# A decoder layer on eight cores: from tile-by-tile through all stages to three passes over the sequence

## The chip, the cores and the metric

The kernel runs on all 8 cores of one Trainium2 chip, two dies of four cores (0 to 3 and 4 to 7). Each core works on half a sequence: 32 blocks of 128 tokens, and one block before them (the halo) that the attention and the pooling look back on. The metric is the device time in microseconds of the slowest core.

The runs also show a slower state: the granted TensorE clock is lower, mostly on one die, and the run is longer (in one run after 2931 us against 2684, with one die at a clock of 0.828 to 0.856 and the other at 0.935 to 0.961). Runs are therefore marked fast or slow.

## The reference, cut to what matters

```python
D_MODEL, BATCH, SEQ, D_FF = 1024, 4, 8192, 2816      # WINDOW = BLOCK = 128

mod = (silu(c) @ w_ada + b_ada).reshape(b, 9, 1024)  # shift, scale, gate of 3 sub-layers
# FFN, half step
h = modulate(x, sh1, sc1)                            # LayerNorm * (1 + scale) + shift
y = (silu(h @ w_gate) * (h @ w_up)) @ w_down
x = layer_norm(ALPHA * x + 0.5 * g1 * y, ln1_g, ln1_b)
# mixer: sliding-window attention with sinks, beside causal pooling over 2, 4, 8, 16 tokens
h = modulate(x, sh2, sc2)
x = layer_norm(ALPHA * x + g2 * token_mix(h), ln2_g, ln2_b)
# FFN, half step, with its own weights
h = modulate(x, sh3, sc3)
x = layer_norm(ALPHA * x + 0.5 * g3 * swiglu(h), ln3_g, ln3_b)
```

Inputs and weights are float32. In both kernels all large multiplications are in bfloat16.

## The kernel before

A helper records each operation with the buffers that it reads and writes, and turns that into semaphore waits. Each engine carries out its own operations in the recorded order (in e1 below VectorE stood 52.3 us behind one load). Below, PE stands for TensorE (matmuls; PEld are its weight loads), DVE for VectorE, ACT for ScalarE, POOL for GpSimd and SP for SyncE, which here only issues transfers. HBM is the memory that the inputs and the `scr_` copies lie in (492 MB were read from it). PSUM is the memory that the matmuls write to (the tiles `ps`, `tp` and `modps` of the profile); an operation of another engine that reads a result out of it is called an evacuation.

The kernel takes a tile of four blocks (512 tokens) through all three sub-layers before the next tile. Stage A is the first FFN (of the next tile), L the mixer, C the second FFN.

```python
order = [("A", 0)]
for t in range(NT):                      # NT = 9: the halo block, then 8 tiles
    if t + 1 < NT:
        order.append(("A", t + 1))
    order.append(("L", t))
    if t > 0:
        order.append(("C", t))
```

The kernel does not keep the weights of the three stages on chip together: every stage loads its own. At the start they are cast to bfloat16 copies in HBM. From there the gate/up weights go through a ring of two buffers. The down weights and the mixer weights take turns in one region.

```python
def issue_gu(upto):                      # gate/up: 1 MB per group, 11 groups per stage
    ...
    P.op("sp", lambda e, ...: e.dma_start(out=wgu[s][:], in_=scr_gu[f][j]), ...)
def load_wd_slot(f, j): ...              # down: 0.5 MB, 11 per stage
def load_mixer_w(): ...                  # 4.5 MB per tile
...
def cast_dma(dst, src, sem, bufs):       # f32 in HBM -> bf16 in HBM
    P.op("pool", lambda e, ...: e.dma_start(out=dst, in_=src), writes=bufs, dma=sem)
```

The attention mask is added before exp by a second matmul into the same PSUM buffer:

```python
e.matmul(ps[pb]..., lhsT=kT[...], rhs=qT_v[...], start=True, stop=False)
return e.matmul(ps[pb]..., lhsT=ident_bf[:], rhs=masks[:, mi, :]..., start=False, stop=True)
...
P.op("act", lambda e, ...: e.activation(out=E_v[iE][:, kv, jj, :], in_=ps[pb][:], func=AF.Exp, scale=0.125), ...)
```

The softmax here doesn't subtract the row's maximum and nothing guards it: scores larger than these inputs give would overflow.

Of the kernel before, what the change touches and what calls it, by code (L numbers as in the profile page):

```python
# [12 lines left out]
D = 1024  # L13
FF = 2816
NFC = 22
NGRP = 11
SEQ = 8192
NB_OWN = 32
TOK_OWN = 4096
TOK_IN = TOK_OWN + 128  # L20
# [3 lines left out]
NEG = -30000.0  # L24
POOL_WINDOWS = (2, 4, 8, 16)
ENG = ("pe", "act", "dve", "pool", "sp")

class Buf:
    def __init__(self, name, overlaps=()):
        self.name = name  # L30
        self.last_w = None
        self.readers = {}
        self.overlaps = list(overlaps)

class Prog:
    def __init__(self, nc, es):
        self.nc = nc
        self.es = es
        self.sems = {}
        for e in ENG:  # L40
            self.sems[e] = es.enter_context(nc.semaphore("s_" + e))
        self.cnt = {e: 0 for e in ENG}
        self.dcnt = {}
        self.q = {e: [] for e in ENG}
        self.waited = {e: {} for e in ENG}

    def new_sem(self, name):
        self.sems[name] = self.es.enter_context(self.nc.semaphore(name))
        self.dcnt[name] = 0
        return name  # L50

    def op(self, eng, fn, reads=(), writes=(), dma=None, waits=()):
        need = {}

        def add(ev):
            if ev is None:
                return
            k, v = ev
            if need.get(k, 0) < v:
                need[k] = v  # L60
# [3 lines left out]
        for b in writes:  # L64
            add(b.last_w)
            for k, v in b.readers.items():
                add((k, v))
            for o in b.overlaps:
                add(o.last_w)
                for k, v in o.readers.items():  # L70
                    add((k, v))
# [3 lines left out]
        for k, v in need.items():  # L75
            if k == eng and eng == "pe":
                continue
            if self.waited[eng].get(k, 0) >= v:
                continue
            self.waited[eng][k] = v  # L80
            wl.append((k, v))
# [15 lines left out]
    def flush(self, block):  # L97
        qs = self.q
        self.q = {e: [] for e in ENG}
        sems = self.sems  # L100

        def mk(eng):
            def body(e):
                for wl, fn, ev in qs[eng]:
                    for k, v in wl:
                        e.wait_ge(sems[k], v)
                    ins = fn(e)
                    ins.then_inc(sems[ev[0]], 1 if ev[0] in ENG else 16)
# [7 lines left out]

def build_program():
# [4 lines left out]

    x_c = din("x_c", [TOK_IN, D])
    c_c = din("c_c", [128, 8])
    w_ada = din("w_ada", [D, 9 * D])
    b_ada = din("b_ada", [1, 9 * D])
    wg = [din("ffn1_w_gate", [D, FF]), din("ffn2_w_gate", [D, FF])]
    wu = [din("ffn1_w_up", [D, FF]), din("ffn2_w_up", [D, FF])]
    wdn = [din("ffn1_w_down", [FF, D]), din("ffn2_w_down", [FF, D])]
    lng_d = [din("ln1_g", [1, D]), din("ln2_g", [1, D]), din("ln3_g", [1, D])]  # L130
    lnb_d = [din("ln1_b", [1, D]), din("ln2_b", [1, D]), din("ln3_b", [1, D])]
    w_in = din("w_in", [D, 1280])
    sinks_d = din("sinks_b", [128, 8])
    wmix_d = din("pool_w_mix", [4, 128, 128])
    pscale_d = din("pool_scale_p", [128, 4])
    w_out = din("w_out", [D, D])
    ident_bf_d = din("ident_bf", [128, 128], BF16)
    ident_f_d = din("ident_f", [128, 128])
    masks_d = din("masks", [128, 3, 128], BF16)
    amat_d = din("amat", [128, 16, 128], BF16)  # L140
    out_c = nc.dram_tensor("out_c", [TOK_OWN, D], F32, kind="ExternalOutput").ap()

    scr_gu = [nc.dram_tensor(f"scr_gu{f}", [NGRP, 128, 8, 2, 256], BF16).ap() for f in range(2)]
    scr_d = [nc.dram_tensor(f"scr_d{f}", [128, NFC, D], BF16).ap() for f in range(2)]
    scr_win = nc.dram_tensor("scr_win", [128, 8, 1280], BF16).ap()
    scr_woa = nc.dram_tensor("scr_woa", [128, 4, D], BF16).ap()
    scr_wop = nc.dram_tensor("scr_wop", [128, 4, D], BF16).ap()

    with ExitStack() as es:
        P = Prog(nc, es)  # L150

        def sb(name, shape, dt=F32, stack=es):
            return stack.enter_context(nc.sbuf_tensor("t_" + name, list(shape), dt))

        ident_bf = sb("ident_bf", [128, 128], BF16)
        ones_bf = sb("ones_bf", [128, 64], BF16)
        masks = sb("masks", [128, 3, 128], BF16)
        amat = sb("amat", [128, 16, 128], BF16)
        wmix = sb("wmix", [128, 4, 128], BF16)
        pscale = sb("pscale", [128, 4])  # L160
        sinkexp = sb("sinkexp", [128, 8])
        sinkb = sb("sinkb", [128, 4, 128])
        lng = [sb(f"lng{i}", [128, D]) for i in range(3)]
        lnb = [sb(f"lnb{i}", [128, D]) for i in range(3)]
        gate3 = sb("gate3", [128, D])
        msc = sb("msc", [128, 6, 8])

        B_const = Buf("const")
        B_gates = Buf("gates")
        B_msc = Buf("msc")  # L170
        B_sink = Buf("sink")

        s_const = P.new_sem("d_const")

        with ExitStack() as pes:
            ct = sb("ct", [128, 8], F32, pes)
            ident_f = sb("ident_f", [128, 128], F32, pes)
            cs = sb("cs", [128, 8], F32, pes)
            crep = sb("crep", [128, 8, 128], BF16, pes)
            ones_f = sb("ones_f", [1, 128], F32, pes)  # L180
            bada = sb("bada", [1, 9 * D], F32, pes)
            modb = sb("modb", [128, 9 * D], F32, pes)
            wada_t = [sb(f"wada{i}", [128, 8, 256], BF16, pes) for i in range(4)]
            dtmp = sb("dtmp", [128, 8, 128], F32, pes)
            gates = [sb(f"gate{i}", [128, D], F32, pes) for i in range(3)]
            stg_in = [sb(f"stg_in{i}", [128, 2, D], F32, pes) for i in range(3)]
            stg_out = [sb(f"stg_out{i}", [128, 2, D], BF16, pes) for i in range(3)]
            B_si = [Buf(f"si{i}") for i in range(3)]
            B_so = [Buf(f"so{i}") for i in range(3)]
            s_si = [P.new_sem(f"d_si{i}") for i in range(3)]  # L190
            s_so = [P.new_sem(f"d_so{i}") for i in range(3)]
            modps = [pes.enter_context(nc.psum_tensor(f"modps{i}", [128, 512], F32)) for i in range(2)]
            B_modps = [Buf(f"modps{i}") for i in range(2)]
            B_wada = [Buf(f"wada{i}") for i in range(4)]
            s_wada = [P.new_sem(f"d_wada{i}") for i in range(4)]
            B_modb = Buf("modb")
            B_misc = Buf("misc")
            B_dtmp = Buf("dtmp")

            cast_fam = {"gu0": [], "gu1": [], "win": []}  # L200
            for f in range(2):
                cast_ops = cast_fam[f"gu{f}"]
                for j in range(NGRP):
                    for gu, wsrc in enumerate((wg[f], wu[f])):
                        src = wsrc.rearrange("(kc p) (j n) -> j p kc n", p=128, n=256)[j]
                        dst = scr_gu[f][j][:, :, gu, :]
                        cast_ops.append((dst, src))
            cast_fam["wd2"] = []
            for j in range(NGRP):
                cast_fam["wd2"].append((scr_d[1][:, 2 * j:2 * j + 2, :],  # L210
                                        wdn[1].rearrange("(fc p) d -> p fc d", p=128)[:, 2 * j:2 * j + 2, :]))
            w_in_v = w_in.rearrange("(kc p) n -> p kc n", p=128)
            cast_ops = cast_fam["win"]
            cast_ops.append((scr_win[:, :, 512:1280], w_in_v[:, :, 512:1280]))
            for kc in range(8):
                for half in range(2):
                    src = w_in[kc * 128:(kc + 1) * 128, half * 256:(half + 1) * 256].rearrange("p (c d) -> p c d", d=64)
                    dst = scr_win[:, kc, 0:512].rearrange("p (c h d) -> p c h d", h=2, d=64)[:, :, half, :]
                    cast_ops.append((dst, src))
            cast_ops.append((wmix[:], wmix_d.rearrange("g c d -> c g d")))  # L220
            const_loads = [
                (ident_bf[:], ident_bf_d), (ident_f[:], ident_f_d), (masks[:], masks_d), (amat[:], amat_d),
                (pscale[:], pscale_d), (sinkexp[:], sinks_d), (ct[:], c_c), (bada[:], b_ada),
            ]
            for i in range(3):
                const_loads.append((lng[i][:], lng_d[i].partition_broadcast(128)))
                const_loads.append((lnb[i][:], lnb_d[i].partition_broadcast(128)))
# [302 lines left out]
        def drain():  # L530
            while live:
                tick()
# [375 lines left out]
```

## Time and profile before

| | before |
|---|---|
| time, median of 3 runs | 3764.38 us (3759.59 to 3768.85) |
| granted clock, median of each die | 0.861, 0.863 |
| PE busy | 70% of the span |

The page of the profiled execution: first the PE's busy time with its share and number of instructions, then rows of 40 equal slices of the span. Each digit is a share in tenths (9 is 90% or more); PEclk is the granted TensorE clock.

```profile
PE 2633.0 (70%) x12252; PEld 1204.5 (32%) x12252; DVE 1025.5 (27%) x1807; ACT 939.4 (25%) x1560; POOL 360.0 (10%) x284
...
PE   5601247478489858986799669966997699759567
...
PEclk9997568789699978997899879987998799879778
DMA  9869999942044304430443134313341235113122
```

The first eight slices, 750 us, have full DMA rows and gaps in PE. After them PE and its clock rise and fall with every tile.

The busy table by stage of the same core. The columns are the stretch in us, its length, busy us and instruction count of PE, PEld, DVE, ACT, POOL, then the granted clock, the share of the DMA engines and GB/s. The first five rows are one steady tile (A: gate/up, down; L; C: gate/up, down); the last two are the start.

```profile
core 3: us, PE busy (x) PEld busy (x) DVE busy (x) ACT busy (x) POOL busy (x), PEclk, DMA share, GB/s
1174.00:1252.00 78.00, 71.15 (x320) 31.47 (x320) 15.71 (x23) 13.67 (x22) 4.55 (x5) 0.98 0.70 243
1252.00:1306.00 54.00, 42.60 (x202) 19.78 (x203) 23.41 (x51) 17.23 (x30) 7.04 (x3) 0.90 0.19 75
1306.00:1424.00 118.00, 65.79 (x320) 28.60 (x318) 32.72 (x65) 45.57 (x79) 13.80 (x9) 0.72 0.10 38
1424.00:1515.00 91.00, 82.32 (x384) 37.49 (x384) 21.38 (x36) 28.02 (x39) 0.00 (x0) 0.94 0.48 177
1515.00:1562.60 47.60, 46.74 (x209) 20.76 (x210) 25.65 (x40) 8.51 (x14) 7.96 (x5) 0.96 0.16 50
0.00:535.00 535.00, 163.95 (x796) 99.55 (x796) 75.94 (x103) 44.46 (x93) 83.25 (x103) 0.83 0.96 164
535.00:782.00 247.00, 137.85 (x592) 60.53 (x592) 41.21 (x74) 39.34 (x64) 25.71 (x27) 0.76 0.93 169
```

The mixer is the worst stage of the tile: PE is busy 66 of 118 us at a clock of 0.72. The waits of PE (the tile that it waited to fill or read, the engine and operation that ended the wait, total us, times, longest) name what it stands for:

```profile
PE tp L473 <- ACT t_n2b L461: 218.0, 3, 138.3
PE tp L473 <- ACT t_n2b L434: 187.0, 9, 21.2
PE ps L553 <- DMA t_wgu<-scr_gu: 170.0, 23, 17.9
PE tp L473 <- ACT t_hTa L479: 125.6, 54, 5.1
PE ps L690 <- ACT t_u L682: 115.2, 24, 7.6
PE ps L698 <- ACT t_u L693: 57.4, 32, 3.1
PE tp L473 <- ACT t_hTb L479: 46.6, 24, 2.2
```

L473 are the transposes between stages, L690 and L698 the pool-mix and output matmuls, L553 gate/up. Within these lines the weight stream (`t_wgu`) has 170 us, of which 149 us lie before 782 us. The waits between and inside stages (all lines but the weight stream and the first, which is the start) add up to 532 us, of which 23 lie before 782 us.

### The profile page before, as it was taken

The page shows a single profiled execution, that of the slowest core. Times are in us where ns is not written, and L with a number is a line of the kernel's source. Part 1 is how long each engine was busy: PE and PEld are TensorE (multiplying, and loading weights), DVE is VectorE, ACT ScalarE, POOL GpSimd, SP SyncE. Part 2 cuts the span into 40 slices and gives each one's busy share as a digit, 9 for nine tenths or more (in the row PEclk, how much of TensorE's full clock was granted, in tenths as well). Part 3 has the DMA queues.
Part 4 walks back from the last instruction along what each step waited for, and adds up shares of the span by engine and source line. Part 5 has one row for each costly group of instructions (what it writes and reads, how often), then busy time and mean ns, then how long its engine had stood idle before and what let it go on. Part 6 is the DMA issues. An engine that isn't in the chain of part 4 may idle for free.

```text
span 3762.5 us, 35982 instructions; the slowest of 8 cores (3733.4 to 3762.5 us)
## 1 busy us (share of the span) xinstructions
PE 2633.0 (70%) x12252; PEld 1204.5 (32%) x12252; DVE 1025.5 (27%) x1807; ACT 939.4 (25%) x1560; POOL 360.0 (10%) x284
## 2 busy tenths in 40 slices
PE   5601247478489858986799669966997699759567
PEld 2301223133144323432344234432443244324223
DVE  0230011213323332333233223322322332233223
ACT  0001021123321233123312341233213321431421
POOL 1101211100101010100010001010101000000001
PEclk9997568789699978997899879987998799879778
DMA  9869999942044304430443134313341235113122
GB/s 176 101 204 164 170 177 191 163 166 97 27 179 151 129 13 166 161 137 18 149 153 118 67 123 155 142 67 123 116 182 68 106 113 202 68 50 145 62 99 81
DMA packets 176277, 468.29 MB, mean 124 GB/s; under 512 B 19553, under 2 KB 102753, under 8 KB 148705
## 3 DMA queue, kind: packets, MB, share of 16 engines
q1 hardware_dynamic: 64002, 356.26, 27.0%
q0 software_dynamic: 109936, 101.85, 16.4%
q10 hardware_dynamic: 2160, 7.87, 0.5%
q8 instruction: 102, 1.67, 0.2%
q14 instruction: 77, 0.63, 0.1%
HBM read 491.76 MB, written 56.10 MB: 146 GB/s over the span
## 4 chain that ended last, share of the span: by engine, by line
PE 59%; DMA 10%; DVE 8%; ACT 8%; issue 6%; POOL 2%; DVEq 0%; ACTq 0%; SPq 0%; POOLq 0%
PE ps L553 30%; PE ps L578 15%; DVE t_stt L419 4%; DMA scr_gu<-ffn_w_gate 4%; DMA t_wgu<-scr_gu 3%; PE ps L698 3%; ACT t_hTa L479 2%; PE ps L596 2%; PE tp L473 2%; PE ps L701 2%; PE ps L617 2%; ACT t_hTb L479 1%; DMA t_rbuf<-x_c 1%; POOL t_xt L511 1%; DMA t_u<-scr_d 1%
## 5 line engine op out<-in xcount | busy, mean ns | idle before, releaser
L553 PE MATMUL ps<-t_hTa,t_wgu 128*128 128x512 bf16 (+1 forms) x3168 | 670.9, 378 | 177.5 <-DMA t_wgu<-scr_gu 169.1
L578 PE MATMUL ps<-t_u 128*128 128x512 bf16 x2860 | 646.4, 390 | 75.5 <-issue 44.5
L553 PE MATMUL ps<-t_hTb,t_wgu 128*128 128x512 bf16 x2816 | 632.7, 388 | 18.0 <-ACT t_hTb L479 16.7
L561 DVE TENSOR_TENSOR t_u<-ps,t_sg 128x512 bf16<-128x512 f32 (+1 forms) x374 | 250.0, 668 | 1375.0 <-ACT t_sg L559 1355.1
L473 PE MATMUL tp<-t_ident_bf,t_n2b 128*128 128x128 bf16 x784 | 92.4, 289 | 577.2 <-ACT t_n2b L461 218.0
L559 ACT ACTIVATE t_sg<-ps 128x512 bf16<-128x512 f32 (+1 forms) x374 | 216.2, 578 | 1088.8 <-PE ps L553 1086.0
L553 PEld LDWEIGHTS ps<-t_hTa,t_wgu 128*128 128x128 bf16 x3168 | 314.5, 104 | 532.5 <-issue 218.3
L578 PEld LDWEIGHTS ps<-t_u 128*128 128x128 bf16 x2860 | 284.4, 100 | 437.3 <-issue 120.0
L553 PEld LDWEIGHTS ps<-t_hTb,t_wgu 128*128 128x128 bf16 x2816 | 279.6, 100 | 366.9 <-issue 53.7
L511 POOL TENSOR_TENSOR t_xt<-t_rbuf,t_lnb 128x1024 f32<-128x1024 f32 x65 | 152.4, 2345 | 1716.8 <-DVE t_rbuf L502 1505.0
L473 PEld LDWEIGHTS tp<-t_ident_bf,t_n2b 128*128 128x128 bf16 x784 | 70.5, 129 | 603.0 <-issue 599.7
L499 ACT ACTIVATE t_rbuf<-t_rbuf,t_rs 128x1024 f32<-128x1024 f32 x97 | 120.1, 1238 | 416.3 <-DVE t_rs L429 416.3
L493 DVE TENSOR_TENSOR t_rbuf<-ps,t_xt 128x512 f32<-128x512 f32 x130 | 89.9, 691 | 409.4 <-PE ps L701 234.5
L505 POOL TENSOR_TENSOR t_rbuf<-t_rbuf,t_lnb 128x1024 f32<-128x1024 f32 x32 | 75.0, 2342 | 1149.6 <-DVE t_rbuf L502 1131.4
L502 DVE TENSOR_TENSOR t_rbuf<-t_rbuf,t_lng 128x1024 f32<-128x1024 f32 x97 | 119.6, 1233 | 146.0 <-ACT t_rbuf L499 109.4
L698 PE MATMUL ps<-t_u 128*128 128x512 bf16 x256 | 106.6, 562 | 57.4 <-ACT t_u L693 57.4
L419 DVE BATCH_NORM_STATS2 t_stt<-t_rbuf 128x6 f32<-128x512 f32 x194 | 134.3, 692 | 12.1 <-DVE t_stt L419 0.5
L479 ACT ACTIVATE t_hTa<-tp,t_msc 128x512 bf16<-128x512 bf16 (+1 forms) x144 | 106.7, 741 | 75.9 <-PE tp L473 68.9
L254 PE MATMUL modps<-t_wada,t_crep 128*128 128x256 bf16 x288 | 67.3, 413 | 56.5 <-DVE t_crep L236 30.6
L596 PE MATMUL ps<-t_hTa,t_u 128*128 128x512 bf16 (+1 forms) x328 | 85.1, 427 | 30.6 <-ACT t_hTa L479 15.6
L419 DVE BATCH_NORM_STATS2 t_stt<-t_xt 128x6 f32<-128x512 f32 x130 | 89.7, 690 | 47.1 <-POOL t_xt L511 40.4
L434 ACT ACTIVATE t_n2b<-t_xt,t_rs 128x1024 bf16<-128x1024 f32 x65 | 78.0, 1235 | 92.2 <-DVE t_rs L429 92.2
(85 smaller groups left out, 1690.2 us busy)
## 6 DMA issues: line engine op xcount, KB each, us to landing
t_wgu<-scr_gu SPq DMA_DIRECT2D x187, 1024.0 KB, 6.0
t_u<-scr_d SPq DMA_DIRECT2D x187, 512.0 KB, 6.9
t_u<-scr_win SPq DMA_DIRECT2D x9, 2560.0 KB, 9.2
t_wada<-w_ada POOLq DMA_DIRECT2D x36, 512.0 KB, 11.0
t_rbuf<-x_c POOLq DMA_DIRECT2D x33, 512.0 KB, 5.3
t_xt<-x_c POOLq DMA_DIRECT2D x8, 2048.0 KB, 19.0
out_c<-t_rbuf POOLq DMA_DIRECT2D x32, 512.0 KB, 3.2
t_stg_in<-ffn_w_down SPq DMA_DIRECT2D x22, 512.0 KB, 6.3
```

The lines of the kernel that those rows point to most:

```text
L419: P.op("dve", lambda e, h=h: e.bn_stats(out=st_t[:, b, h, :], in_=src_ap[:, h * 512:(h + 1) * 512]), reads=[B_src], writes=[B_s])
L473: ins = e.transpose(out=tp[:, j, b * 128:(b + 1) * 128], in_=n2b[b][:, kc * 128:(kc + 1) * 128], identity=ident_bf[:])
L479: P.op("act", lambda e, j=j, kc=kc: e.activation(out=hdst[:, kc, 0:T], in_=tp[:, j, 0:T], func=AF.Identity, scale=msc[:, 2 * mi + 1, kc:kc ...
L499: P.op("act", lambda e: e.activation(out=r[:], in_=r[:], func=AF.Identity, scale=rs[:, b, 0:1], bias=rs[:, b, 1:2]), reads=[B_r[b], B_st[b ...
L502: P.op("dve", lambda e: e.tensor_tensor(out=r[:], in0=r[:], in1=lng[li][:], op=ALU.mult), reads=[B_r[b], B_const], writes=[B_r[b]])
L511: P.op("pool", lambda e: e.tensor_tensor(out=xt[par][:, b, :], in0=r[:], in1=lnb[li][:], op=ALU.add), reads=[B_r[b], B_const], writes=[B_x ...
L553: ins = e.matmul(ps[pb][:, 0:T], lhsT=wgu[slot][:, kc, gu, s2 * 128:(s2 + 1) * 128], rhs=hsrc[:, kc, 0:T], start=(kc == 0), stop=(kc == 7))
L559: P.op("act", lambda e, pg=pg, isg=isg: e.activation(out=sg[isg][:, 0:T], in_=ps[pg][:, 0:T], func=AF.Silu), reads=[B_ps[pg]], writes=[B_s ...
L561: P.op("dve", lambda e, pu=pu, isg=isg, fc=fc: e.tensor_tensor(out=aT_v[:, fc, 0:T], in0=ps[pu][:, 0:T], in1=sg[isg][:, 0:T], op=ALU.mult) ...
L578: ins = e.matmul(ps[4 + h][:], lhsT=aT_v[:, fc, b * 128:(b + 1) * 128], rhs=wd_v[:, fc, h * 512:(h + 1) * 512], start=(fc == 0), stop=(fc ...
L596: ins = e.matmul(ps[pb][:, 0:T], lhsT=win_v[:, kc, c * 128:(c + 1) * 128], rhs=hsrc[:, kc, 0:T], start=(kc == 0), stop=(kc == 7))
L698: e.matmul(ps[2 + h][:], lhsT=attn_v[b % 2][:, c, :], rhs=woa_v[:, c, h * 512:(h + 1) * 512], start=(c == 0), stop=False)
```

## The change

The intent: go over the sequence three times (first FFN, mixer, second FFN). In each pass all its weights sit in one on-chip region of 33 pages, loaded once. The activations go from pass to pass through HBM. The bfloat16 copies in HBM disappear; the weights arrive by casting loads straight into the pages. The gates are multiplied into the down weights, the pool-mix matrix into the output weights. The mask becomes a factor of 0 or 1 after exp. Almost the whole file is rewritten; the core of it, with cuts:

```diff
-    scr_gu = [nc.dram_tensor(f"scr_gu{f}", [NGRP, 128, 8, 2, 256], BF16).ap() for f in range(2)]
-    scr_d = [...]; scr_win = ...; scr_woa = ...; scr_wop = ...
+    scr_x1 = nc.dram_tensor("scr_x1", [NBLK, 128, D], F32).ap()
+    scr_n2 = nc.dram_tensor("scr_n2", [NBLK, 128, D], BF16).ap()
+    scr_x2 = nc.dram_tensor("scr_x2", [NOWN, 128, D], F32).ap()
+    scr_g = nc.dram_tensor("scr_g", [3, D], F32).ap()
...
+    W = sb("W", [128, NPAGE * PG], BF16)            # 33 pages of 128 x 2048
+    ps = es.enter_context(nc.psum_tensor("ps", [128, 8, 512], F32))   # 4 pairs of buffers, taken in turn
...
+    def cast_gu(f, fc, waits=()):                   # one page, f32 -> bf16 on the way in
+        p = gu_page(f, fc)
+        P.op("pool", lambda e: e.dma_start(out=W[:, p * PG:(p + 1) * PG], in_=wgu_d[f][fc]), writes=[B_page[p]], ...)
...
+    def gate_rows(i, eng):                          # gate as a column per partition -> a row on all partitions
+        ...
+        P.op(eng, st, reads=[B_gcol], writes=[B_sg_d[i]], dma=s_gcol)      # 1024 elements of 4 bytes to HBM
+        P.op(eng, lambda e: e.dma_start(out=gate[:], in_=scr_g[i:i + 1, :].partition_broadcast(128)), ...)
...
-                e.matmul(ps[pb]..., lhsT=kT[...], rhs=qT_v[...], start=True, stop=False)
-                return e.matmul(ps[pb]..., lhsT=ident_bf[:], rhs=masks[:, mi, :]..., start=False, stop=True)
+                ins = e.matmul(ps[:, 2 * pr + kv, :]..., lhsT=kT[...], rhs=qT[...], start=True, stop=True)
...
+            P.op("act", lambda e, ...: e.activation(out=E_v[iE][:, jj, :, :], in_=ps[:, 2 * pr:2 * pr + 2, :], func=AF.Exp, scale=0.125),
+                 reads=[B_ps[pr]], writes=[B_E[iE]])
+            P.op("dve", lambda e, ...: e.tensor_tensor(out=ev, in0=ev, in1=masks[:, mi, :]..., op=ALU.mult),
+                 reads=[B_E[iE], B_am], writes=[B_E[iE]])
...
+    lanes["w"].append(mods(0, 24, cb0, B_lngb, 4))  # conditioning: 24 chunks now, 48 later
+    finish_lane("w")
+    for fc in range(NFC):
+        cast_gu(0, fc, ...)
+    gate_rows(0, "act")
+    transpose_round(0, kns0, 0)
+    transpose_round(1, kns0, 0)
+    lanes["w"].append(fold_down(0, 0, NFC))         # down weights * gate row, on VectorE
+    ...
+    ffn(0, tiles0, kns0, g_hook0, d_next0)          # tiles of 4, 3, 2, then six of 4 blocks
+    ...                                             # mixer, 32 blocks, software-pipelined
+    ffn(1, tiles1, kns1, g_hook1, lambda b: None)
```

## The prediction

> **What bounds the kernel now.** TensorE, badly fed. In the chain of waits PE holds 59% of the 3762 us span (gate/up 30%, down 15%), DMA 10%, VectorE 8%, ScalarE 8%. By stage:
>
> 1. Start. In the busy table by stage the first full FFN tile starts at 535 us; until 782 us DMA is 93 to 96% busy (casting f32 weights into bf16 copies in HBM, then streaming them back), PE busy 302 of 782 us. The chain has 11 links of 8 to 15 us that are gate-weight casts.
> 2. A steady tile of 512 tokens: 388 us (1174 to 1562): first FFN 78 + 54, mixer 118, second FFN 91 + 48. The chain shows 352 gate/up matmuls in 77.9 us and 176 down matmuls in 39.85 us, so two FFNs need 235 us. In the mixer PE is busy 66 of 118 us at a granted clock of 0.72; its largest waits are 20.9 us for normalised rows before a transpose and 21.6 us for pooling evacuations.
> 3. Every tile reloads the weights (356 MB on the SP-fed queue); PE waits 170 us for gate/up tiles, mostly early.
>
> **What the change does.** It removes the bf16 copies, the reloads, the mask matmuls (128 of 390 ns) and the pool-mix matmuls. It adds x1, n2, x2 through HBM (under 2 MB per 128-token block and pass, some 60 GB/s where 200 to 280 have been seen: hidden), residual reloads, and mask multiplies on VectorE (two per block, about 1 us each, estimate). VectorE work in an FFN pass comes to about 14 us per block against 29.4 of PE; in the mixer VectorE and ScalarE take about 8 us each against 11 to 12. PE stays the limit.
>
> **Sum** (estimates from these durations):
> - Start: about 51 MB of f32 must land before the first down projection. The conditioning weight now streams 37.7 MB in 155 us, 243 GB/s, hence 215 us; gate/up starts near 60 us, DMA-paced; first tile ends at 255.
> - Rest of pass 1: 29 blocks x 29.4 + 30 (transposes, tile edges) = 885.
> - Pass change (f32 fold matmuls, tables): 25.
> - Mixer: 33 x 14 = 460.
> - Pass 3: 32 x 29.4 + 35 = 977.
> - Tail 12; collisions on the in-order VectorE and SP queues 60.
>
> 2675 us at full clock. The start gives about 400 us of the gain, the steady tiles the rest, mostly the mixer and the stalls between stages.
>
> **Clock risk.** [...] from 3360 to 3440 us all eight cores have PE 96% busy at clock 0.98 to 1.00. But dense stretches here are under 250 us; the change makes them a thousand. One chance in four that a lowered clock shows in the usual runs[...]; the point moves up a little for it.
>
> **Predicted: 2710 us, range 2590 to 3050.** Faster by over 2%: 0.97; within 2%: 0.015; slower: 0.015.
>
> **What would show it.** Right: PE at 9 or 10 tenths with clock 1.0 through both FFN passes, about 118 us per four-block tile; DMA busy only in the first 220 us; no gate/up wait on weights after the first tile; mixer blocks near 14 us. Wrong: PE waiting for fold loads past 300 us; mixer blocks over 18 us waiting for ScalarE or VectorE (softmax denominators, masks); clock near 0.8 in dense stretches.
>
> **What would make it wrong.** The clock; VectorE blocked in order behind a weight load; cast loads slower than 243 GB/s; the mixer's rotating PSUM pairs serialising on evacuations.

The sum: it came to 2675 us (the terms as printed add to 2674), and 35 us on top, for the risk of a lowered clock, make 2710. Those 35 us and the one chance in four were the author's estimate, as were the terms of 25, 12 and 60 us.

## The result, and the profile after

| | before | after |
|---|---|---|
| time, median of 4 runs | 3761.99 us (3757.55 to 3768.85) | 2683.62 us (2680.43 to 2931.41) |
| ratio of fast runs | | 0.7131 (95%: 0.7112 to 0.7149) |
| granted clock, median of each die | 0.861, 0.863 | 0.960, 0.961 |
| PE busy | 70% | 86% |
| HBM read | 492 MB | 217 MB |

A ratio is the mean time of one kernel's fast runs over that of the other's in the same rounds, so it is not quite the ratio of the medians. One of the four runs after was slow: 2931 us, with one die at a clock of 0.828 to 0.856.

The page after, in the same lines as before:

```profile
PE 2296.9 (86%) x11652; PEld 1085.1 (41%) x11652; DVE 1206.0 (45%) x1853; ACT 579.5 (22%) x880; POOL 352.3 (13%) x406
...
PE   0079888999999999877777776499999999999997
...
PEclk7589998999999999888888898799999999999998
DMA  8955754121302112533444423451121111112100
```

The three passes are plain to see: full PE rows with a clock of 9 tenths, then the mixer at 7 to 8, then full rows again to the end. The first two slices have no matmul but 32 transposes of 3.6 us in all.

The chain of waits of the kernel after, in order of time (start, us, what), through the start and one steady FFN tile:

```profile
71.80 22.11 DMA t_xs<-adaT
95.93 47.36 DMA scr_g<-t_gcol
...
143.80 0.79 ACT t_hT L489
150.82 78.91 PE ps L504 x352
...
573.12 75.97 PE ps L504 x352
649.09 9.50 PE ps L517 x44
658.59 0.89 PE ps L484 x16
659.48 9.50 PE ps L517 x44
668.98 0.89 PE ps L484 x16
669.87 18.99 PE ps L517 x88
```

A full tile is 75.97 + 4 x 9.50 + 2 x 0.89 = 115.75 us of matmuls and transposes with nothing between them. That is 215.8 ns per matmul of 512 columns; the prediction had used 221 and 226 ns from the kernel before, which has gaps between its groups. The first tile is another matter: its gate/up matmuls start at 151 us, held up by ScalarE's first `t_hT` evacuation, which itself followed a transfer of `t_gcol` that took 47 us. That transfer in turn could be issued only at 96 us, behind the loads of the conditioning weight (`t_xs<-adaT`).

The waits of PE after:

```profile
PE ps L504 <- ACT t_hT L489: 128.1, 2, 124.3
...
PE ps L484 <- DVE t_n L410: 23.0, 1, 23.0
PE ps L690 <- ACT t_aT L625: 22.3, 1, 22.3
...
PE ps L484 <- ACT t_aT L625: 16.3, 1, 16.3
...
```

No matmul waits for a weight load any more, and the transposes' large waits (L484 here) are gone, but for one of 23.0 us at the very start and one of 16.3 us at the end of the mixer. What is left is the start (124.3 us in one wait), the pass changes, and the mixer, whose steady period is 61.2 us per four blocks where the kernel before needed 118.

Where the time fell, roughly: the kernel before had taken five blocks through the first FFN by 783 us, the kernel after by about 301 us (interpolated between four blocks at 269 and seven at 366). So about 480 us of the 1083 us between the two profiled spans come from the start, and 600 us from all that follows. The busy table over all that follows, before and then after (columns as above), splits the 600:

```profile
782.00:3762.00 2980.00, 2331.21 (x10864) 1044.38 (x10864) 908.35 (x1630) 855.57 (x1405) 250.99 (x154) 0.87 0.31 114
301.00:2679.00 2378.00, 2146.09 (x10892) 1011.25 (x10892) 1072.19 (x1644) 544.27 (x827) 323.88 (x357) 0.95 0.27 83
```

PE is busy 185 us less and idle 417 us less (649 us before, 232 after). Part of the gain is thus shorter work of PE itself: the mask and pool-mix matmuls are gone, and the granted clock is 0.95 instead of 0.87.

### The profile page after: what moved, and what is told of

Read it like the earlier page. It is cut to its first block, busy times and chain, and to the rows that moved or that the text cites. A ratio compares the mean times of both kernels' runs of the same rounds, so it can differ in the third digit from the quotient of the medians.

```text
span 2678.9 us, 33222 instructions; the slowest of 8 cores (2666.4 to 2678.9 us)
## 1 busy us (share of the span) xinstructions
PE 2296.9 (86%) x11652; PEld 1085.1 (41%) x11652; DVE 1206.0 (45%) x1853; ACT 579.5 (22%) x880; POOL 352.3 (13%) x406
## 4 chain that ended last, share of the span: by engine, by line
PE 73%; DMA 8%; DVE 6%; ACT 6%; issue 5%; POOL 1%; DVEq 0%; ACTq 0%; SPq 0%; POOLq 0%
PE ps L504 42%; PE ps L517 23%; DMA scr_g<-t_gcol 3%; PE ps L586 3%; DMA t_xs<-adaT 3%; ACT t_hT L489 2%; ACT t_aT L625 2%; PE ps L604 2%; DVE t_stt L401 1%; PE ps L484 1%; DVE t_aT L629 1%; POOL t_rs L406 1%; PE ps L690 1%; DMA t_xs<-scr_x 1%; DVE t_sg L648 1%
## 5 line engine op out<-in xcount | busy, mean ns | idle before, releaser
L504 PE MATMUL ps<-t_hT,t_W 128*128 128x512 bf16 (+2 forms) x5984 | 1258.9, 373 | 169.8 <-ACT t_hT L489 128.1
L504 PEld LDWEIGHTS ps<-t_hT,t_W 128*128 128x128 bf16 x5984 | 590.4, 99 | 836.1 <-issue 190.6
L517 PE MATMUL ps<-t_W,t_aT 128*128 128x512 bf16 x2860 | 624.8, 379 | 1.3 <-DVE t_aT L509 1.3
L509 DVE TENSOR_TENSOR t_aT<-ps,t_sg 128x512 bf16<-128x512 f32 (+2 forms) x374 | 248.5, 666 | 617.7 <-ACT t_sg L508 616.3
L508 ACT ACTIVATE t_sg<-ps 128x512 bf16<-128x512 f32 (+2 forms) x374 | 216.2, 578 | 1293.1 <-PE ps L504 849.0
L406 POOL TENSOR_TENSOR t_rs<-t_rs,t_mhalf 128x1 f32<-128x1 f32 x195 | 176.6, 906 | 1887.7 <-DVE t_rs L405 1868.9
L517 PEld LDWEIGHTS ps<-t_W,t_aT 128*128 128x128 bf16 x2860 | 278.4, 98 | 332.0 <-issue 1.9
L401 DVE BATCH_NORM_STATS2 t_stt<-t_xs 128x6 f32<-128x512 f32 x382 | 264.3, 692 | 61.7 <-DMA t_xs<-scr_x 24.9
L489 ACT ACTIVATE t_hT<-ps,t_msc 128x512 bf16<-128x512 bf16 (+3 forms) x208 | 156.5, 753 | 424.4 <-PE ps L484 281.8
L690 PE MATMUL ps<-t_W,t_aT 128*128 128x512 bf16 x512 | 128.9, 410 | 23.7 <-ACT t_aT L625 22.3
L586 PE MATMUL ps<-t_hT,t_W 128*128 128x512 bf16 (+1 forms) x328 | 89.2, 433 | 41.8 <-ACT t_aT L594 24.5
L629 DVE TENSOR_TENSOR t_aT<-t_aT 128x1024 bf16<-128x1024 bf16 x64 | 46.7, 730 | 135.5 <-ACT t_aT L625 135.5
L484 PE MATMUL ps<-t_ident,t_n 128*128 128x128 bf16 x784 | 56.5, 230 | 59.8 <-DVE t_n L410 23.0
L690 PEld LDWEIGHTS ps<-t_W,t_aT 128*128 128x128 bf16 x512 | 51.7, 104 | 88.3 <-issue 42.1
L484 PEld LDWEIGHTS ps<-t_ident,t_n 128*128 128x128 bf16 x784 | 51.6, 104 | 70.4 <-issue 61.6
L625 ACT ACTIVATE t_aT<-ps 128x1024 bf16<-128x1024 f32 x64 | 65.2, 1020 | 59.8 <-DVE t_aT L629 59.1
```

What stands on the lines that cost most here:

```text
L401: P.op("dve", lambda e, h=h: e.bn_stats(out=stt[:, s, h, :], in_=src[:, h * 512:(h + 1) * 512]), reads=[B_src], writes=[B_st[s]])
L406: P.op("pool", lambda e: e.tensor_tensor(out=rs[:, s, 1:2], in0=rs[:, s, 0:1], in1=mhalf[:], op=ALU.pow), reads=[B_st[s], B_ones], writes= ...
L484: ins = e.transpose(out=tv[:, j, b * 128:(b + 1) * 128], in_=n_t[kns[b]][:, kc * 128:(kc + 1) * 128], identity=ident[:])
L489: P.op("act", lambda e, j=j, kc=kc: e.activation(out=hT[:, kc, 0:nb * 128], in_=tv[:, j, 0:nb * 128], func=AF.Identity, scale=msc[:, 3 * m ...
L504: ins = e.matmul(ps[:, 2 * pr + gu, 0:T], lhsT=W[:, o:o + 128], rhs=hT[:, kc, 0:T], start=(kc == 0), stop=(kc == 7))
L508: P.op("act", lambda e: e.activation(out=sgt[:, i, 0:T], in_=ps[:, 2 * pr, 0:T], func=AF.Silu), reads=[B_ps[pr]], writes=[B_sg[i]])
```

## The experiments

All but e14 and e6 change the kernel after; those two change the kernel before. They are told in this order: the start (two), the crowded small tiles (one), the mask (five), the weight stream (two), and two versions that put the findings together. Each ratio is to the kernel before, run on the same chip; the kernel after has 0.7131.

### e1: the first gate row issued from SP

```diff
-        gate_rows(0, "act")
+        gate_rows(0, "sp")
```

> The first gate row's two transfers are issued from SP instead of ScalarE; nothing else changes. Theory (in-order ScalarE): the first gate/up matmuls waited until 151 us because ScalarE could not evacuate the transposed rows before a 4 KB transfer of 47 us had landed. Then the first gate/up group starts near 103 us, the first tile ends near 225 us instead of 269, and the time falls by 35 to 50 us, to about 2640. Rival (the start is bound by bytes, as my prediction had it): gate/up starts early but waits page by page for the weight casts, and the down projection waits for the folds; the first tile still ends past 255 us and the time stays above 2670.

Only one of five runs was fast: 2666 us, where the kernel after takes 2683. The profiled run was slow, so only its order and its long waits are read here; in the stretch right after, from 160 to 270 us, its clock was 1.00. The PE's timeline at the start, each line with the idle time before it in brackets:

```profile
67.31 15.60 PE L504 MATMUL ps<-t_hT,t_W 128*128 128x512 bf16 x63 [40.09 <-ACT t_hT L489]
99.14 1.44 PE L504 MATMUL ps<-t_hT,t_W 128*128 128x512 bf16 x3 [16.23 <-DVE t_aT L509]
...
153.86 6.33 PE L504 MATMUL ps<-t_hT,t_W 128*128 128x512 bf16 x16 [44.89 <-DVE t_aT L509]
```

and VectorE's largest wait in that stretch:

```profile
DVE t_W L360 <- DMA t_xs<-wdn: 52.6, 2, 52.3
```

Gate/up starts at 67 us, earlier than the theory said, and then stops twice. The second stop, 44.9 us, is for VectorE: its next recorded operation is the first fold of a down weight, whose load stands on SP behind the gate row's round trip through HBM. So freeing ScalarE was not enough. The same slow transfer blocked ScalarE before (126.1 us idle) and blocks VectorE now (52.3 us), since each works in order. The first tile ended at 252 us. Both theories had the size wrong; the first had the cause of the late start right.

### e2: gate rows through PE, not through HBM

```diff
-            P.op(eng, st, reads=[B_gcol], writes=[B_sg_d[i]], dma=s_gcol)
-            P.op(eng, lambda e: e.dma_start(out=gate[:], in_=scr_g[i:i + 1, :].partition_broadcast(128)), ...)
+            P.op("dve", lambda e: e.tensor_tensor(out=gv, in0=gcol[:].unsqueeze(2).to_broadcast([128, 8, 128]),
+                                                  in1=ident[:].unsqueeze(1).to_broadcast([128, 8, 128]), op=ALU.mult), ...)
+            # 2 f32 matmuls: ones[128,128] x gate[:, h*512:(h+1)*512] -> every partition holds the row
+            P.op("dve", lambda e: e.tensor_copy(out=gate[:], in_=ps[...]), ...)
```

> All three gate rows are spread over the partitions by a VectorE product with the identity and two f32 matmuls against ones, so no gate row goes through HBM. Theory (the gate rows' small transfers block the queues that they are issued from, at the start and at both pass changes): gain of the start as in the other run or a little more, 45 us, plus 15 to 20 us at the change to the mixer and 20 to 25 us at the change to the last pass: about 2600 (2575 to 2620). Rival (the pass changes are bound by handing x2 on through HBM and by the normalising chain): only the start gains, 2630 to 2650, and PE still idles some 60 us around the change to the last pass.

Measured: 2623 and 2626 us in its two fast runs, ratio 0.6960 (0.6932 to 0.6989) against 0.7131. The timeline of PE at the start:

```profile
101.08 3.75 PE L358 MATMUL ps<-t_gate,t_onesf 128*128 128x512 f32 x4 [101.08 <-DVE t_gate L351]
...
113.71 77.61 PE L512 MATMUL ps<-t_hT,t_W 128*128 128x512 bf16 x352 [6.24 <-ACT t_hT L497]
```

Gate/up starts at 114 us and runs through without a stop, so neither the weight casts nor the folds hold it: the DMA-paced gate/up of the prediction is refuted. What comes before 98 us is still a chain of conditioning loads (`t_xs<-adaT`), which no run tried to shorten. Passing 4 KB per pass through HBM cost about 60 us in all, some 38 us of it at the start and the rest at the two pass changes. It came out just above the expected range (2575 to 2620), so the pass changes gave less than expected.

### e3: the later conditioning chunks moved to a later tile

```diff
         def start_rest():
-            load_lngb(0)
             ...
             if t == 0 and fc == 6:
+                load_lngb(0)
+            if t == 3 and fc == 6:
                 lanes["w"].append(start_rest())
```

> The 48 conditioning chunks for the later sub-layers start in the fourth tile of pass 1 instead of the first. Theory (they crowd VectorE while the 3-block and 2-block tiles run, 134 of 188 us busy, and PE waits for gate/up products): the stretch of 188 us for five blocks shrinks to about 155, total about 2650 (2640 to 2660), and the later full tiles stay at 116 us because VectorE is under half busy there. Rival (the small tiles themselves lose the time: fewer columns per weight load, more normalising work per matmul): within 10 us of 2683.

Measured: 2668.5 to 2669.8 us in three fast runs, ratio 0.7079 (0.7059 to 0.7100). The stretch of the two small tiles fell from 186 to 164 us. At 115.75 us per four blocks it should be 145. The next two full tiles rose to 118.7 and 117.5 us. So the crowding of VectorE is about half of the loss in this stretch, the small tiles themselves are the rest, and part of what was gained came back as cost later. The net gain, about 14 us, lies between the two theories.

### e4: the mask as a matmul again

```diff
-                        ins = e.matmul(ps[:, 2 * pr + kv, :]..., lhsT=kT[...], rhs=qT[...], start=True, stop=True)
+                        e.matmul(ps[:, 2 * pr + kv, :]..., lhsT=kT[...], rhs=qT[...], start=True, stop=False)
+                        ins = e.matmul(ps[:, 2 * pr + kv, :]..., lhsT=ident[:], rhs=masks[:, mi, :]..., start=False, stop=True)
...
-                P.op("dve", lambda e, ...: e.tensor_tensor(out=ev, in0=ev, in1=masks[:, mi, :]..., op=ALU.mult), ...)
...                                       # the mask constants become 0 and -30000
```

> The mask goes back to an additive matmul before exp, as in the kernel before; the VectorE multiply goes. Theory (in the mixer the PE stream counts): 128 more matmuls at 216 to 320 ns add 25 to 40 us: about 2715. Rival (the mixer is bound by the chain of evacuations, and the multiply of 0.73 us sits in that chain between exp and the attention matmul): the two cancel, within 12 us of 2683.

Measured: 2642.6 to 2646.0 us in three fast runs, ratio 0.7013 (0.6992 to 0.7034). It is 38 us faster than the kernel after, though PE does 128 matmuls more. Both theories failed, in sign. That raised a new question: is the multiply dear, or do added matmuls help by keeping PE's clock up? A stretch of the steady mixer of the kernel after, then of this one, in the busy table (columns as above):

```profile
1301.00:1546.00 245.00, 186.25 (x1120) 86.93 (x1120) 110.58 (x162) 123.02 (x177) 64.78 (x64) 0.90 0.45 121
```

```profile
1296.00:1520.00 224.00, 203.25 (x1168) 93.03 (x1188) 90.68 (x129) 125.36 (x177) 75.28 (x66) 0.98 0.48 132
```

Four tiles took 245 us and now 224, and the clock rose from 0.90 to 0.98. Both explanations fit that.

### e9 and e10: no mask at all, and both masks

e9 leaves the multiply out and adds no matmul (wrong). e10 keeps the multiply and adds the matmul of e4 with its own additive mask (right, masked twice).

> The kernel after without any mask, neither multiplied nor added: wrong on purpose. The run with the mask on PE was 38 us faster than the kernel after although PE does 128 more matmuls. Theory (the multiply stands in the chain from exp to the attention matmul and in VectorE's order, and PE waits for it): without either the mixer is at least as fast as with the mask on PE, up to 30 us faster for the matmuls saved: 2615 to 2645. Rival (the extra matmuls help by keeping PE busy, so that its clock is granted more of the time: 0.97 instead of 0.89 in a steady mixer stage): without them the mixer stays slow, 2660 or more.

> The kernel after with both: the additive mask matmuls on PE and, after exp, the multiply on VectorE; the result is right. Theory of the chain: the multiply still stands in the chain and PE has more to do, so 2683 to 2715. Rival of the clock: the added matmuls fill PE's gaps, its clock is granted more, and the time falls below 2675 with the multiply in place.

Measured: e9 2608.5 to 2629.3 us in four fast runs, ratio 0.6935 (0.6880 to 0.6990). It passed the comparison with the reference all the same, so that comparison does not test the mask; nothing is claimed of e9's values. e10 2699.8 to 2707.9 us in three, ratio 0.7162 (0.7116 to 0.7208). The four make a square:

| | no added matmul | added matmul | the matmul costs |
|---|---|---|---|
| multiply on VectorE | 0.7131 (after) | 0.7162 (e10) | 0.0031, 12 us |
| no multiply | 0.6935 (e9) | 0.7013 (e4) | 0.0078, 29 us |
| the multiply costs | 0.0196, 74 us | 0.0149, 56 us | |

(Differences of ratios, times 3770 us.) With the intervals above, each difference is good to some 20 us, so the 12 us are not distinct from zero. There is a second caution. e9 and e10 ran on the second chip. Up to the mixer the four kernels are alike, yet the third tile starts at 476 us in e9 and e10 and at 456 and 457 us in after and e4. From there to the end of the profiled span, which leaves this difference out, after takes 2223 us, e10 2223, e9 2152 and e4 2184. So the multiply costs 72 us without the added matmul and 38 with it; the matmul costs 32 us without the multiply and nothing with it. In neither row does the added matmul save time, so its effect on the clock does not explain e4: that rival is refuted. e10 shows it plainest. Its steady mixer, then that of e9, in the busy table:

```profile
1303.00:1549.00 246.00, 212.04 (x1181) 94.34 (x1180) 109.63 (x161) 123.85 (x176) 64.40 (x64) 0.94 0.46 119
...
1300.00:1540.00 240.00, 207.77 (x1272) 99.23 (x1297) 103.34 (x147) 143.01 (x206) 79.72 (x72) 0.93 0.58 143
```

In e10 four tiles take 246 us at a clock of 0.94, where the kernel after takes 245 at 0.90: more clock and no time gained. e9 is faster than both at 0.93. The mixer's period per four blocks follows: 61.2 us after, 61.6 in e10, 51.1 in e9, about 56 in e4. The multiply costs about as much as its own 46.7 us of busy time (64 of 0.73 us) or more, although VectorE is busy only 111 of 245 us, so something waits for it. The timeline of the kernel after, around one block, shows what (VectorE and ScalarE lines only):

```profile
1338.11 1.02 ACT L625 ACTIVATE t_aT<-ps 128x1024 bf16<-128x1024 f32 x1
...
1339.22 0.69 DVE L629 TENSOR_TENSOR t_aT<-t_aT 128x1024 bf16<-128x1024 bf16 x1 [1.50 <-ACT t_aT L625]
...
1340.01 1.02 ACT L625 ACTIVATE t_aT<-ps 128x1024 bf16<-128x1024 f32 x1 [0.89 <-DVE t_aT L629]
1341.14 0.69 DVE L629 TENSOR_TENSOR t_aT<-t_aT 128x1024 bf16<-128x1024 bf16 x1 [1.22 <-ACT t_aT L625]
...
1343.54 0.68 DVE L648 TENSOR_TENSOR t_sg<-ps,t_small 128x512 f32<-128x512 f32 x1
1344.32 0.63 ACT L651 ACTIVATE t_sg<-t_sg 128x512 f32<-128x512 f32 x1 [3.28 <-DVE t_sg L648]
```

L625 is exp, L629 the multiply. The second exp waits for the first multiply, though they touch different halves of the tile: the program gives both halves one name (`B_E[iE]`), so its bookkeeping orders them. And the softmax denominator (L648), for which PE had been done since 1339, comes only at 1343.54, behind both multiplies and what follows them on VectorE.

### e13: the multiply on GpSimd

```diff
-                P.op("dve", lambda e, ev=ev, mi=mi: e.tensor_tensor(out=ev, ...
+                P.op("pool", lambda e, ev=ev, mi=mi: e.tensor_tensor(out=ev, ...
```

> The kernel after with the mask multiply moved from VectorE to GpSimd. With and without the added matmul the VectorE multiply cost 56 to 74 us for 47 us of busy time. If what costs is the length of the chain exp, multiply, attention matmul: the multiply takes about 2 us on GpSimd and waits behind its other work, so 2700 or more. If what costs is VectorE's in-order queue (denominators and evacuations stand behind a multiply that waits for exp): VectorE is freed, and the time falls below 2665.

Measured: 2715 to 2726 us in four fast runs, ratio 0.7206 (0.7173 to 0.7240), by the ratios 28 us slower than with VectorE (25 from the third tile to the end). The multiply took 2.13 us on GpSimd. VectorE was freed of it and that did not help; the theory that freeing VectorE pays is refuted. That the longer chain from exp to the attention matmul is what hurt is likely, but e13 doesn't single it out: GpSimd also has the normalising steps to do, and ScalarE's waits for them (`t_rs`) rose from 23 to 52 us. How much of it is the shared name of the two halves was not tried; that the split of the name would bring a good part of it back is argued, not shown.

### e14: the multiply alone, in the kernel before

```diff
-                        e.matmul(ps[pb]..., lhsT=kT[...], rhs=qT_v[...], start=True, stop=False)
-                        return e.matmul(ps[pb]..., lhsT=ident_bf[:], rhs=masks[:, mi, :]..., start=False, stop=True)
+                        return e.matmul(ps[pb]..., lhsT=kT[...], rhs=qT_v[...], start=True, stop=True)
...
+                    P.op("dve", lambda e, ...: e.tensor_tensor(out=ev, in0=ev, in1=masks[:, mi, :]..., op=ALU.mult), ...)
...                                       # the mask constants become 1 and 0
```

> The kernel before with this one part of the change alone: mask matmuls out, the multiply after exp in (four of 128x512 per block on VectorE). Theory (as in the kernel after, the multiply costs more than the matmuls that it saves): slower by 10 to 50 us, 3775 to 3815 against 3765. Rival (in the kernel before scores run a block ahead, so the chain has slack, and 41 us of matmuls are saved): faster by 15 to 40 us.

Measured: 3836 and 3842 us in its two fast runs, ratio 1.0172 (1.0104 to 1.0241). The verdict by the 2% rule is unclear, but the interval excludes any gain. This one part of the change alone costs the kernel before about 65 us, a little beyond the expected range. The four exps of a block and the four multiplies share one name here too.

### e5: residency taken away from the kernel after

```diff
+        def again(f, p):      # a page back from a bf16 copy in HBM, behind ScalarE's silu of the same group
+            P.op("act", lambda e: e.dma_start(out=W[:, p * PG:(p + 1) * PG], in_=scr_w[f][p]), ...)
...
                     gateup(f, fc, nb * 128)
+                    if t == 0:
+                        keep(f, gu_page(f, fc))          # written to HBM once
+                    elif not last:
+                        again(f, gu_page(f, fc))
+                    ...                                  # likewise the down pages
```

> The kernel after, but the weights are not resident in effect: in each FFN pass every weight page is written once to HBM as bf16 and loaded again for each following tile, from the ScalarE queue right behind an instruction that already waited for the page's last matmul. That is 17 MB per tile, as the kernel before did. Theory (the reload was mostly hidden and the gain comes from the stages): the full FFN tile stays at 116 to 118 us and the time at 2683 to 2715. Rival (residency is the gain): the tile goes back to the 130 us or more of the kernel before, the time over 2850.

Measured: 2761 to 2785 us in four fast runs, ratio 0.7329 (0.7263 to 0.7396): 75 us slower. Neither figure held. The chain of waits through a steady tile:

```profile
636.99 75.97 PE ps L507 x352
712.97 9.50 PE ps L520 x44
...
733.75 18.99 PE ps L520 x88
```

With the lines left out, which repeat 9.50 and twice 0.89 as in the kernel after, the steady tile is 115.75 us (from 636.99 to 752.74), unchanged to the hundredth, with 17 MB per tile streaming under it at a DMA share of 0.62. The loss lies where loads are short in any case: the third tile starts at 518 us instead of 456, and by the second tile of the last pass 83 us have been lost. Some 20 us of both have nothing to do with the reload (on the same chip e9 and e10, which have none, start the third tile at 476), so the reload cost about 60. It was fully hidden in steady tiles, and cost time where the fold and conditioning loads compete with it.

### e6: the steady weight stream taken away from the kernel before

```diff
+                if i >= 2 * NGRP:            # gate/up: only the first two stages load
+                    gu_state["issued"] += 1
+                    continue
+            if gu_state["cons"] > 2 * NGRP:  # down; mixer weights likewise
+                return
...                                      # later matmuls name all weight buffers of the shared region
```

> The kernel before with its steady weight loads left out: after the first two FFN stages no gate/up, down or mixer weight is loaded again, so later tiles compute with stale weights and the result is wrong on purpose. Theory (the reload was mostly hidden): the time falls only by the waits on weight loads of the steady tiles, some 40 us, and a little at the start where loads shared the DMA engines with the background casts: 3680 to 3740; the tile of 388 us stays above 375. Rival (residency is the gain): it falls by 300 us or more.

The result is wrong (stale weights). Measured: 3685 to 3688 us in three fast runs, ratio 0.9761 (0.9712 to 0.9811). The tile goes from 385.5 us (1515.49 to 1901.00, between two like points in the chain of waits) to 375.6 (1490.15 to 1865.71). The steady stream was worth 90 us: within the range (3680 to 3740), though twice the 40 us of waits that it was reckoned from, and far from the 300 of the rival. So of the 1078 us that the change gained, some 8% is the reloading that resident weights save. What residency does for the start, where the bfloat16 copies in HBM fall away, was not tried alone.

### e11 and e12: the findings together

e11 is e2, e3 and e4 in one kernel. e12 adds that in the mixer VectorE evacuates half of the transposed rows:

```diff
+                if mi == 1 and j >= 2:
+                    P.op("dve", lambda e, j=j, kc=kc: e.tensor_scalar(out=hT[:, kc, 0:nb * 128], in0=tv[:, j, 0:nb * 128],
+                                                                      scalar1=msc[...], scalar2=msc[...], op0=ALU.mult, op1=ALU.add), ...)
+                    continue
```

> Three edits together on the kernel after: gate rows through PE (60 us faster alone), the mask as an additive matmul (38 us), the later conditioning chunks from the fourth tile (14 us). If the three gaps are separate places in time the gains add: about 2571 (2555 to 2590). If they fill one another's gaps, 2595 or more.

> The same, and in the mixer every second pair of transposed rows is evacuated by VectorE instead of ScalarE. Theory (PE's last large wait in a steady mixer stage with the mask on PE, 2.5 us per four blocks for a PSUM pair held by ScalarE's eight evacuations in a row, and as much again behind it, is a ScalarE burst): 10 to 25 us faster than the run without it. Rival (VectorE's order is the tighter one, as the mask multiply showed): no gain, or slower.

Measured: e11 2559 to 2587 us in six fast runs, ratio 0.6808 (0.6770 to 0.6847). The sum of the single gains was 2571, so the three gaps are separate places. e12 2535.7 to 2564.6 us in five fast runs, ratio 0.6759 (0.6721 to 0.6798). The two intervals overlap, so by the times alone the step from e11 to e12 is likely, not proven; the mixer's period fell from about 56 to 52.0 us per four blocks in the profiled runs. Over eight tiles that would be 32 us, and the means of the fast runs differ by 18 (2568 and 2551), so not all of it reached the end. The PE line and slices of e12's page:

```profile
PE 2326.5 (92%) x11792; PEld 1094.0 (43%) x11792; DVE 1189.4 (47%) x1832; ACT 558.4 (22%) x844; POOL 360.8 (14%) x406
...
PE   0399989999999999988999996999999999999996
```

e12 beats both kernels: about 5% under the kernel after.

## Why the prediction was right, and where it was not

The time was right: 2710 predicted, 2684 measured, and the sum at full clock, 2675, is closer still. But that it came out so close is luck: the mixer's term was 71 us too small, the two FFN passes 42 and 45 us too large, and they made up for each other. The sum as predicted against the profile after (points of the chain of waits and the PE timeline):

| term | predicted | measured |
|---|---|---|
| start to the end of the first tile | 255 | 269 |
| rest of pass 1, with 60 for collisions | 945 | 903 (269 to 1172) |
| pass change and mixer | 485 | 556 (1172 to 1728) |
| pass 3 | 977 | 932 (1728 to 2659) |
| tail | 12 | 20 |

- **PE stays the limit in the FFN passes: right.** The block is 28.9 us rather than 29.4, and the 30 to 35 us per pass for transposes and edges were not needed in steady tiles (a transpose round is 0.89 us). This term was too high by 45 us in pass 3.
- **Nothing waits for weights after the first tile: right**, by the waits of PE.
- **The start: right in size by luck, wrong in mechanism.** "gate/up starts near 60 us, DMA-paced" failed. It started at 151 us, then ran at full speed. What held it was ScalarE, in order behind the conditioning loads until 96 us and then behind a 4 KB transfer of 47 us; without that transfer (e2) it started at 114 us and the first tile ended at 231. The transfer's 1024 elements of 4 bytes took 47.4 us from issue to landing, beside the weight casts; the same at the two pass changes took 18.1 and 16.8 us. The prediction had not seen `gate_rows(0, "act")` as anything but small.
- **Mixer: mis-sized.** "Mixer: 33 x 14" was 15.3 us per block in the steady part, plus PE waits of 22.3 and 16.3 us at its end. The multiply was costed by its own time, "about 1 us each" (0.73 measured), and taken as free because VectorE had slack. The runs show a cost of 56 to 74 us by the ratios (38 to 72 from the third tile on): engines and PE wait for it. Without any mask the block is 12.8 us, with the mask on PE about 14.
- **Collisions of 60 us: right in size only.** The two small tiles lost 41 us, of which e3 puts about half down to VectorE's order, and the last tile of pass 1 lost 20 us (136 against 115.75).
- **"DMA busy only in the first 220 us": wrong, and harmless.** The DMA share was still 0.6 until 456 us and 0.2 to 0.5 in the mixer.
- **The clock: right for the usual run.** In the profiled fast run all eight cores had 0.99 to 1.00 in the full tiles of both FFN passes: for 463 us (573 to 1036) and again for 808 us (1850 to 2658) PE was 98% busy or more on each core, at a granted clock of 1.00. So dense matmuls on all cores did not by themselves lower it there. One run in four was slow, with one die at 0.828 to 0.856. In the profiled slow run of e1, whose cores had 0.899 to 0.912 over the whole span, a group of 49 matmuls on core 6 took 10.74 us until 2168 us and 13.04 us from 2182 us to the end of the last pass. What sets this off stays open.
- **Where the gain comes from.** "The start gives about 400 us": about 480. No run took this apart in the kernel before; its chain of waits runs through casts of gate and up weights into HBM until 460 us (`scr_gu<-ffn_w_gate`, `scr_gu<-ffn_w_up`) and through the loads back, which the kernel after doesn't have. The rest is some 600, of which 185 is shorter work of PE and 417 shorter waits. The steady weight stream is 90 of it (e6), and the new mask form takes about 40 away (e4). What remains of the shorter waits, at least some 330, I put down to the order of stages: in the kernel before PE waited 532 us between and inside stages, and in three passes the work it needs next is long done. That is a difference of measured numbers and a reading of the waits. No run undid the order alone, so it is argued, not shown.

The traces show engines held by their own order: in e1 VectorE stood 52.3 us behind one load, and PE waited 44.9 us for it to empty PSUM; in the kernel after ScalarE's first `t_hT` evacuation had 126.1 us of idle time before it, until the 47.4 us transfer had landed.

## What to carry to other kernels

Cost an operation by what stands behind it in its engine's order and in its chain, not by its busy time: a 0.73 us multiply cost more than the matmul it replaced, and a 4 KB transfer held all of the first tile. When a loop is reordered, reckon the waits that it removes as well as the traffic: here PE's waits after the start fell by 417 us, and the saved traffic was worth 90. And before a small difference between runs of two chips is put down to an edit, look at a stretch that the edit doesn't touch: here 20 us of it lay there. When an engine that computes also issues a transfer that waits for another transfer, ask which of its later operations PE needs first.
